# Two heads at a time in SSD and retention, and whole-row products for the last 16 tokens, in a two-layer hybrid decoder trunk

## Chip, cores and metric

The kernel runs on one core of one Trainium2 chip. The metric is device time in microseconds (us), the median of the runs shown. TensorE (PE) does the matrix products; VectorE (DVE), ScalarE (ACT) and GpSimd (POOL) work on tiles; SyncE (SP) issues most loads.

## What is computed

Two layers over 272 tokens (16 learned meta tokens and 256 of the input) of width 1024, all in float32 for its user. Each layer norms its input, projects it, runs four causal token mixers side by side, gates and sums their branch projections, and ends with an out projection and a squared-ReLU MLP. Cut to what matters here:

```python
for l in range(DEPTH):                          # 2
    u = rms_norm(h, norm_pre_mix[l])
    proj = u @ w_in[l]
    y_ret  = retention_mixer(...)   # 4 heads, keys of 64, values of 128, rotary on q and k, fixed decay
    y_s5   = s5_mixer(...)          # 32 groups of 16 channels, 64 complex states each
    y_ssd  = ssd_mixer(...)         # 8 heads of 64 channels in 2 groups, keys of 128, decay from the data
    y_hg   = hgrn2_mixer(...)       # 4 heads, keys and values of 128, a decay for each key channel
    mixed = sum(sigmoid(gate) * branch_projection) @ w_out[l]
    h = h + rms_norm(mixed, norm_post_mix[l])
    m = square(relu(rms_norm(h, norm_pre_mlp[l]) @ w_up[l])) @ w_down[l]
    h = h + rms_norm(m, norm_post_mlp[l])
return h[:, N_META:]
```

For a head with a scalar decay a mixer is y[t] = sum over s <= t of decay(s, t) (q[t] . k[s]) v[s].

## The kernel before

**The stream.** Channels lie on the partitions, tokens along the free dimension. All weights come in 336 chunks of 128 x 1024 in float32 (load on SP, L318). ACT makes the chunk's high part `whi` (L325), DVE its low part `wlo` (L327), both float32r; one chunk gives 24 products, high by high (L344), high by the input's low part (L345), low by high (L347), into one of three banks "g". This stream of products runs through the whole kernel, and what the mixers do comes in between. The chunks of a layer come in the order HGRN2's inputs, SSD's, S5's, gates and branch projections with retention's inputs among them, out projection, MLP.

**The mixers over tokens.** HGRN2, SSD and retention are computed without a recurrence, as a masked 272 x 272 product a head. The tokens are cut into tiles of 128, 128 and 16. `scores` makes k^T q for the three tiles of s against the tokens t from that tile on: 272, 144 and 16 columns, laid side by side as 432. The keys `kpad` are padded with zeros to 384 tokens. `attend` sums v[s]^T P[s, t] over the three tiles: 272, 144 and 16 columns again, the last one with 16 rows of contraction (`v2`, a tile of 16 partitions, and `P[0:16, 416:432]`). float32 products stand as two records each in the trace.

- HGRN2 (`hgrn_in` L1177, `hgrn` L1214) builds P of two heads a tile and attends with 128 value channels.
- SSD (`ssd_in` L1319, `ssd` L1411): a head's decay is itself a product, with 32 rows of the array (L1428, `rows=32`, at row 32 mt); ACT applies Relu and Exp (L1429, L1430), POOL multiplies by the group's masked k^T q (L1431), and `attend` (L1432) gives 64 channels, two heads sharing one bank: `yp[64 * hh:64 * hh + 64]`. DVE adds the skip (L1433).
- Retention (`ret_in` L1465, `ret` L1497): POOL rotates q and k (four products on 32 partitions each, L1482, then L1483, L1486, and L1487 into `kpad`), and PE turns the values to token-major order (`turn`, L694). Heads have 64 rows of keys, two in one tile (L1505); DVE masks (L1507), `attend` (L1509) gives 128 channels.
- S5 (`s5` L1072, `s5_run` L1091) works in four quarters with many small steps on PE, DVE, POOL and ACT; its last step copies its outputs back to channels by tokens (eight copies, L1152) and cuts them in two (L364). POOL and DVE build S5's tables between (L979 to L984, L1003 to L1005).

**What sets the order.** Each engine takes its queue strictly in order. The order within an engine is made at build time by a scheduler that simulates the program, guided by program order and by ranks (`high_priority`) for loads and cuts of chunks; so code that is written in another sequence can move instructions far from it. Two resources tie the mixers together: the two banks "ma" (HGRN2, retention) and the two banks "mb" (SSD, then S5), each handed on in program order, and the 4352-byte slots. In `ssd` the loop over four tiles `mt` takes one bank for the outputs of two heads and one more for each head's scores:

```python
for mt in range(4):
    yp = self.bank("mb")[:, :T]
    for hh in range(2):
        sg = self.bank("mb")[:, :432]
        self.scores(sg, L[hh], R, base=32 * mt, rows=32)
        ...
        self.attend(yp[64 * hh:64 * hh + 64], [v01[:, s, hd] for s in range(2)], v2[:, hd], E)
```

At the start POOL zeroes the padding of `kpad` (L394), and 14 products on those zeros (L398) run on PE while the first loads come in.

## Time and profile before

| | |
|---|---|
| median of 3 runs | 1293.81 us (1292.19 to 1296.15) |
| span of the profiled execution | 1294.5 us, 0.7 above the median |
| PE busy | 1231.3 us (95%) |
| DVE busy | 898.3 us (69%) |
| ACT busy | 695.2 us (54%) |
| POOL busy | 388.4 us (30%) |

The profile is of one execution. Matmuls are pipelined and their ends are modelled, so two products overlap in the trace, and a cost on PE is best read from start to start. In a timeline row the first number is the start in us from the span's start, the second the duration; then engine, line, operation, output <- inputs, for PE the rows * columns of the array, partitions x elements, type and count; a bracket at the end is the idle time before, and what released it.

### The profile page before, as it was taken

To read this page: it belongs to the slowest core of one execution; us is meant where nothing else is said; L and a number is where in the kernel's file an instruction comes from. 1 tells how busy PE (TensorE), PEld (TensorE's weight loads), DVE (VectorE), ACT (ScalarE), POOL (GpSimd) and SP (SyncE) were. 2 spreads that over 40 slices of the span, in tenths; PEclk is the share of its full clock that TensorE was granted. 3 is DMA by queue.
4 is the path that set the end of the run, shared out by engine and by line. 5 is a ranking of instruction groups with operands and counts; after the bars stand their busy time and mean duration, and the time that the engine had idled before them with its cause. 6 is when DMAs were issued, how large, how long until landed. Compare 5 with 4: busy or idle time off the path is not lost.

```text
span 1294.5 us, 24278 instructions
## 1 busy us (share of the span) xinstructions
PE 1231.3 (95%) x9534; PEld 1185.8 (92%) x9534; DVE 898.3 (69%) x1480; ACT 695.2 (54%) x1218; POOL 388.4 (30%) x416
## 2 busy tenths in 40 slices
PE   9999998986999989999989999998999998999997
PEld 8989888885999989999988999998999997999996
DVE  8999958987555775554459795689865486655444
ACT  6446755533465466554445548546536456665442
POOL 2332336686100332210015241265680031322001
PEclk9999999997999999999999999998999999999999
DMA  6423332341345435445443332442343554455552
GB/s 238 154 84 114 112 125 94 103 140 65 115 169 174 172 110 183 172 178 175 170 145 131 121 128 83 154 142 92 115 160 131 188 181 153 153 189 183 188 184 98
DMA packets 53187, 186.69 MB, mean 144 GB/s; under 512 B 6096, under 2 KB 7248, under 8 KB 53072
## 3 DMA queue, kind: packets, MB, share of 16 engines
q1 hardware_dynamic: 50480, 179.40, 40.1%
q10 hardware_dynamic: 2592, 5.74, 1.3%
q8 instruction: 75, 1.23, 0.4%
q14 instruction: 40, 0.33, 0.1%
HBM read 184.06 MB, written 1.05 MB: 143 GB/s over the span
## 4 chain that ended last, share of the span: by engine, by line
PE 70%; DVE 17%; POOL 5%; issue 5%; ACT 2%; DMA 1%; DVEq 0%; SPq 0%; ACTq 0%; POOLq 0%
PE g L347 21%; PE g L345 21%; PE g L344 21%; DVE wlo L327 4%; DMA s5a<-in_bc 1%; DVE S L1152 1%; PE mb L711 1%; POOL S L1482 1%; PE mb L717 1%; DVE S L1395 1%; DVE s5a L1004 1%; DVE h L600 1%; DVE S L1262 1%; PE ma L711 1%; PE ma L717 1%
## 5 line engine op out<-in xcount | busy, mean ns | idle before, releaser
L327 DVE TENSOR_TENSOR wlo<-wst,whi 128x1024 fp32r<-128x1024 f32 x336 | 434.5, 1294 | 244.0 <-PE g L347 209.8
L325 ACT ACTIVATE whi<-wst 128x1024 fp32r<-128x1024 f32 x336 | 355.6, 1059 | 368.8 <-PE g L345 285.4
L347 PE MATMUL g<-xh_u,wlo 128*128 128x272 f32 (+1 forms) x1024 | 301.7, 296 | 16.5 <-DVE wlo L327 16.4
L344 PE MATMUL g<-xh_u,whi 128*128 128x272 f32 (+1 forms) x1024 | 300.3, 294 | 1.3 <-ACT S L654 0.9
L345 PE MATMUL g<-xl_u,whi 128*128 128x272 f32 (+1 forms) x1024 | 298.1, 292 | 0.0
L344 PE MATMUL g<-S,whi 128*128 128x272 f32 (+1 forms) x832 | 236.1, 288 | 4.2 <-ACT S L537 3.7
L347 PE MATMUL g<-S,wlo 128*128 128x272 f32 (+1 forms) x808 | 230.5, 289 | 1.8 <-DVE wlo L327 1.8
L345 PE MATMUL g<-S,whi 128*128 128x272 f32 (+1 forms) x768 | 220.4, 289 | 3.1 <-DVE S L548 3.1
L347 PEld LDWEIGHTS g<-xh_u,wlo 128*128 128x128 f32 x1024 | 196.3, 192 | 20.8 <-DVE wlo L327 18.7
L344 PEld LDWEIGHTS g<-xh_u,whi 128*128 128x128 f32 x1024 | 196.9, 192 | 3.4 <-ACT S L654 1.0
L345 PEld LDWEIGHTS g<-xl_u,whi 128*128 128x128 f32 x1024 | 196.8, 192 | 0.8 <-issue 0.4
L344 PEld LDWEIGHTS g<-S,whi 128*128 128x128 f32 x832 | 157.3, 190 | 5.0 <-ACT S L537 4.2
L347 PEld LDWEIGHTS g<-S,wlo 128*128 128x128 f32 x808 | 152.3, 190 | 2.7 <-DVE wlo L327 2.4
L345 PEld LDWEIGHTS g<-S,whi 128*128 128x128 f32 x768 | 146.0, 190 | 4.9 <-DVE S L548 4.7
L345 PE MATMUL g<-xl_npm,whi 128*128 128x272 f32 (+1 forms) x512 | 148.3, 291 | 2.0 <-DVE xl_npm L548 2.0
L344 PE MATMUL g<-xh_npm,whi 128*128 128x272 f32 (+1 forms) x512 | 143.6, 288 | 2.4 <-ACT xh_npm L537 2.4
L347 PE MATMUL g<-xh_npm,wlo 128*128 128x272 f32 (+1 forms) x496 | 142.6, 288 | 0.0
L345 PEld LDWEIGHTS g<-xl_npm,whi 128*128 128x128 f32 x512 | 98.4, 192 | 2.9 <-DVE xl_npm L548 2.6
L673 POOL TENSOR_TENSOR acc<-acc,tmp 128x272 f32<-128x272 f32 (+1 forms) x48 | 38.0, 807 | 205.4 <-DVE tmp L672 205.4
L344 PEld LDWEIGHTS g<-xh_npm,whi 128*128 128x128 f32 x512 | 96.5, 192 | 3.0 <-ACT xh_npm L537 2.9
L347 PEld LDWEIGHTS g<-xh_npm,wlo 128*128 128x128 f32 x496 | 95.0, 192 | 0.2
L503 POOL TENSOR_TENSOR tmp<-tmp 128x272 f32<-128x272 f32 (+1 forms) x64 | 42.1, 658 | 141.1 <-DVE wlo L327 101.0
(379 smaller groups left out, 2194.4 us busy)
## 6 DMA issues: line engine op xcount, KB each, us to landing
wst<-in_w SPq DMA_DIRECT2D x336, 512.0 KB, 3.5
S<-in_rot ACTq DMA_DIRECT2D x4, 544.0 KB, 5.0
s5a<-in_bc ACTq DMA_DIRECT2D x8, 256.0 KB, 3.7
h<-in_h SPq DMA_DIRECT2D x4, 272.0 KB, 4.8
S<-in_ssdc ACTq DMA_DIRECT2D x2, 384.0 KB, 4.4
dtc<-in_ssdc ACTq DMA_DIRECT2D x2, 272.0 KB, 4.7
out<-h SPq DMA_DIRECT2D x2, 256.0 KB, 2.5
S<-in_lvl SPq DMA_DIRECT2D x1, 448.0 KB, 7.7
```

The costliest lines, as they stand in the source:

```text
L325: a = nc.scalar.activation(hi, st, AF.Copy)
L327: nc.vector.tensor_tensor(out=lo, in0=st, in1=hi.bitcast(F32), op=ALU.subtract)
L344: self.nc.tensor.matmul(out, lhsT=a, rhs=r, start=st, stop=False)
L345: self.nc.tensor.matmul(out, lhsT=a, rhs=s, start=False, stop=False)
L347: end = self.nc.tensor.matmul(out, lhsT=b, rhs=r, start=False, stop=en)
L503: nc.gpsimd.tensor_tensor(out=q, in0=a, in1=a, op=ALU.mult)
L600: e.tensor_tensor(out=self.h[:, k, sl], in0=self.h[:, k, sl], in1=mw[:, k], op=ALU.add)
L673: nc.gpsimd.tensor_tensor(out=a, in0=a, in1=t, op=ALU.add)
L711: nc.tensor.matmul(ps[:, c0:c0 + T - q0], lhsT=k[b, 128 * s:128 * s + 128], rhs=q[b, q0:T], start=True, stop=True)
L717: nc.tensor.matmul(out[:, 0:T], lhsT=v01[0], rhs=P[:, 0:272], start=True, stop=False)
L1004: e.tensor_tensor(out=tmp, in0=X[1 - r], in1=F[1], op=ALU.mult)
L1152: nc.vector.tensor_copy(o, i)
```

## The change

- `scores` and `attend` take several heads at once. The loop over the three token tiles is outside, the heads inside, so that the products of two heads follow each other: on different rows of the array for scores (SSD's 32 rows of two tiles, retention's 64 rows), on different columns for SSD's attends.
- The last 16 tokens go over all 128 rows. `v2` is no longer a tile of 16 partitions but a view of one of two persistent tiles `vpad` (128 x 512), zeroed once by POOL at the start, ahead of `kpad`: the first serves HGRN2 and retention, the second SSD. HGRN2's P gets its columns 416 to 432 zeroed by POOL in each layer.
- `ssd` loops over the two groups and, within, over the two heads of a tile: the scores of two tiles take two banks "mb"; then each tile takes one bank for its outputs. Before, an output bank was taken ahead of the scores.
- `ret` takes two banks "ma" for a pair's scores, and its output banks now from "mb".

Comments are gone as well, so line numbers shift by some 5 to 15.

```diff
+        self.vpad = [self.cp.tile([128, 512], F32, name=f"vpad{i}") for i in range(2)]
+        for t in self.vpad:
+            nc.gpsimd.memset(t, 0.0)
         for t in self.kpad:
             nc.gpsimd.memset(t[:, :, T:384], 0.0)
...
-    def scores(self, ps, k, q, base=0, rows=128):
+    def scores(self, *many, rows=128):
         nc = self.nc
-        b = slice(base, base + rows)
         for s, (c0, q0) in enumerate(((0, 0), (272, 128), (416, 256))):
-            nc.tensor.matmul(ps[:, c0:c0 + T - q0], lhsT=k[b, 128 * s:128 * s + 128], rhs=q[b, q0:T], start=True,
-                             stop=True)
+            for ps, k, q, base in many:
+                b = slice(base, base + rows)
+                nc.tensor.matmul(ps[:, c0:c0 + T - q0], lhsT=k[b, 128 * s:128 * s + 128], rhs=q[b, q0:T], start=True,
+                                 stop=True)
-    def attend(self, out, v01, v2, P):
+    def attend(self, *many):
         nc = self.nc
-        nc.tensor.matmul(out[:, 0:T], lhsT=v01[0], rhs=P[:, 0:272], start=True, stop=False)
-        nc.tensor.matmul(out[:, 128:T], lhsT=v01[1], rhs=P[:, 272:416], start=False, stop=False)
-        nc.tensor.matmul(out[:, 256:T], lhsT=v2, rhs=P[0:16, 416:432], start=False, stop=True)
+        for s, (t, p0) in enumerate(((0, 0), (128, 272), (256, 416))):
+            for out, v01, v2, P in many:
+                nc.tensor.matmul(out[:, t:T], lhsT=v01[s] if s < 2 else v2, rhs=P[:, p0:p0 + T - t], start=s == 0,
+                                 stop=s == 2)
...
-        v01, v2 = self.slot(4, [128, 2, 4, 128]), self.t1([16, 4, 128], tag="v2", bufs=2)
+        v01, v2 = self.slot(4, [128, 2, 4, 128]), self.vpad[0].rearrange("p (i e) -> p i e", i=4)
...
+        for P in PP:
+            g.memset(P[:, :, 416:432], 0.0)
...
-        for mt in range(4):
-            yp = self.bank("mb")[:, :T]
-            EE = self.slot(13 + mt % 2, [128, 2, 432])
+        for gr in range(2):
+            mts = (2 * gr, 2 * gr + 1)
+            EE = [self.slot(13 + mt % 2, [128, 2, 432]) for mt in mts]
             for hh in range(2):
-                hd = 2 * mt + hh
-                sg = self.bank("mb")[:, :432]
-                self.scores(sg, L[hh], R, base=32 * mt, rows=32)
-                E = EE[:, hh]
-                nc.scalar.activation(E, sg, AF.Relu, scale=-1.0)
-                self.decay = nc.scalar.activation(E, E, AF.Exp, scale=-1.0)
-                g.tensor_tensor(out=E, in0=E, in1=sm[:, mt // 2], op=ALU.mult)
-                self.attend(yp[64 * hh:64 * hh + 64], [v01[:, s, hd] for s in range(2)], v2[:, hd], E)
-            v.scalar_tensor_tensor(out=yt[:, mt], in0=xs[:, mt], scalar=self.hf(l, "sd")[:, mt:mt + 1], in1=yp,
-                                   op0=ALU.mult, op1=ALU.add)
+                sg = [self.bank("mb")[:, :432] for _ in mts]
+                self.scores(*[(p, L[hh], R, 32 * mt) for p, mt in zip(sg, mts)], rows=32)
+                for p, ee in zip(sg, EE):
+                    E = ee[:, hh]
+                    nc.scalar.activation(E, p, AF.Relu, scale=-1.0)
+                    self.decay = nc.scalar.activation(E, E, AF.Exp, scale=-1.0)
+                    g.tensor_tensor(out=E, in0=E, in1=sm[:, gr], op=ALU.mult)
+            for ee, mt in zip(EE, mts):
+                yp = self.bank("mb")[:, :T]
+                self.attend(*[(yp[64 * hh:64 * hh + 64], [v01[:, s, 2 * mt + hh] for s in range(2)], v2[:, 2 * mt + hh],
+                               ee[:, hh]) for hh in range(2)])
+                v.scalar_tensor_tensor(out=yt[:, mt], in0=xs[:, mt], scalar=self.hf(l, "sd")[:, mt:mt + 1], in1=yp,
+                                       op0=ALU.mult, op1=ALU.add)
...
-        for hd in range(4):
-            ps = self.bank()[:, :432]
-            self.scores(ps, k[:, hd // 2], q[:, hd // 2], base=64 * (hd % 2), rows=64)
-            P = PP[hd // 2][:, hd % 2]
-            nc.vector.tensor_tensor(out=P, in0=ps, in1=self.c("m432"), op=ALU.mult)
-            yp = self.bank()[:, :T]
-            self.attend(yp, [v01[:, s, hd] for s in range(2)], v2[:, hd], P)
+        for pair in range(2):
+            ps = [self.bank()[:, :432] for _ in range(2)]
+            self.scores(*[(p, k[:, pair], q[:, pair], 64 * i) for i, p in enumerate(ps)], rows=64)
+            for i, p in enumerate(ps):
+                nc.vector.tensor_tensor(out=PP[pair][:, i], in0=p, in1=self.c("m432"), op=ALU.mult)
+            for i in range(2):
+                hd = 2 * pair + i
+                yp = self.bank("mb")[:, :T]
+                self.attend((yp, [v01[:, s, hd] for s in range(2)], v2[:, hd], PP[pair][:, i]))
```

How the order of the built program moves is shown at three places. The first is PE in layer 0, at the first attend of SSD. Before, the products of one head (`mb_1364`; L717 to L719 are its 272, 144 and 16 columns) stand in one place, with two of HGRN2's head norms (L725, L726) among them:

```order
L344 MATMUL g_2409<-xh_u_154,whi_2412 128x272
L717 MATMUL mb_1364<-S_122_1365,S_113_1333 64x272
L718 MATMUL mb_1364<-S_122_1365,S_113_1333 64x144
L725 MATMUL ma_927<-tmp_928,onesr 128x272
L726 MATMUL ma_927<-sq_929,onesr 128x272
L725 MATMUL ma_935<-tmp_936,onesr 128x272
L726 MATMUL ma_935<-sq_937,onesr 128x272
L719 MATMUL mb_1364<-S_122_1365,v_114_1334 64x16
```

In the change a head's 272 columns (`mb_1398`, the same line L726 for all) come 20 rows ahead of this place, alone; here are the second head's 272 and the 144 and 16 columns of both:

```order
L345 MATMUL g_2445<-xl_u_159,whi_2448 128x272
L726 MATMUL mb_1398<-S_119_1368,S_112_1338 64x272
L726 MATMUL mb_1398<-S_119_1368,S_112_1338 64x144 x2
L726 MATMUL mb_1398<-S_119_1368,vpad_92 64x16 x2
L347 MATMUL g_2445<-xh_u_158,wlo_2449 128x272
```

So the attends of a tile are two visits of the stream, with the columns of both heads next to each other in the second one only.

The second place is DVE in layer 0, at the end of S5. Before, the cut of S5's output (L364), the copies back (L1152) and the cuts of chunks (L327) stand in this order:

```order
L1140 TENSOR_TENSOR S_96_1020<-mb_2219,S_200_2200 128x272
L1005 TENSOR_TENSOR s5b_2982<-s5b_2982,s5a_2973 128x4x128
L364 TENSOR_TENSOR S_203_2251<-S_145_1815,S_202_2250 128x272 x2
L327 TENSOR_TENSOR wlo_3486<-wst_3483,whi_3485 128x1024
L1152 COPY S_145_1815<-S_96_1020 32x136 x8
L327 TENSOR_TENSOR wlo_3524<-wst_3521,whi_3523 128x1024
L364 TENSOR_TENSOR S_203_2251<-S_145_1815,S_202_2250 128x272 x2
L327 TENSOR_TENSOR wlo_3561<-wst_3558,whi_3560 128x1024
```

In the change (the copies are L1160):

```order
L1013 TENSOR_TENSOR s5b_2986<-s5b_2986,s5a_2977 128x4x128
L327 TENSOR_TENSOR wlo_3333<-wst_3330,whi_3332 128x1024
L364 TENSOR_TENSOR S_201_2255<-S_143_1819,S_200_2254 128x272 x2
L1160 COPY S_143_1819<-S_95_1025 32x136 x8
L327 TENSOR_TENSOR wlo_3365<-wst_3362,whi_3364 128x1024
L364 TENSOR_TENSOR S_201_2255<-S_143_1819,S_200_2254 128x272
L327 TENSOR_TENSOR wlo_3413<-wst_3410,whi_3412 128x1024
L364 TENSOR_TENSOR S_201_2255<-S_143_1819,S_200_2254 128x272
```

The tail of S5 stands three cuts of chunks earlier in DVE's queue, and a cut stands between its last two pieces.

The third place is POOL in layer 0, around the rotary products of retention. Before (L1482 to L1487 are rotary work, L983, L984 and L1003 to L1005 tables of S5 for the next layer):

```order
L983 TENSOR_TENSOR s5e_2985<-s5ea,s5eb 128x288
L984 TENSOR_TENSOR s5e_2985<-s5e_2985 128x288
L1482 TENSOR_TENSOR S_260_3395<-S_253_3260,S_259_3390 32x1088 x4
L1003 TENSOR_TENSOR s5c_2983<-s5a_2973,s5p 128x4x128
L1004 TENSOR_TENSOR s5d_2984<-s5a_2973,s5p 128x512
L1122 MEMSET s5d_2984 128x8
L1483 TENSOR_TENSOR S_253_3260<-S_253_3260,S_258_3389 128x1088
L1005 TENSOR_TENSOR s5c_2983<-s5c_2983,s5d_2984 128x4x128
L1486 TENSOR_TENSOR S_261_3401<-S_253_3260,S_260_3395 128x544
L1487 TENSOR_TENSOR kpad_89<-S_253_3260,S_260_3395 128x2x272
```

In the change (rotary work is L1496 to L1501, tables L1011 to L1013):

```order
L1011 TENSOR_TENSOR s5c_2987<-s5a_2977,s5p 128x4x128
L1012 TENSOR_TENSOR s5d_2988<-s5a_2977,s5p 128x512
L1130 MEMSET s5d_2988 128x8
L1013 TENSOR_TENSOR s5c_2987<-s5c_2987,s5d_2988 128x4x128
L274 COPY S_256_3393<-S_251_3264 128x1
L274 COPY S_257_3394<-S_251_3264 128x1
L1045 MEMSET s5d_2988 32x4x32
L1045 MEMSET s5d_2988 32x4x64
L1045 MEMSET s5d_2988 32x4x96
L1496 TENSOR_TENSOR S_258_3399<-S_251_3264,S_257_3394 32x1088 x4
L1497 TENSOR_TENSOR S_251_3264<-S_251_3264,S_256_3393 128x1088
L1500 TENSOR_TENSOR S_259_3405<-S_251_3264,S_258_3399 128x544
```

All tables of S5 stand ahead of the rotary products now; before, some stood among them.

## Rows read from the trace of the kernel before

**Rows 1.** The page's first line and its part 1: busy, share, instructions.

```profile
span 1294.5 us, 24278 instructions
...
PE 1231.3 (95%) x9534; PEld 1185.8 (92%) x9534; DVE 898.3 (69%) x1480; ACT 695.2 (54%) x1218; POOL 388.4 (30%) x416
```

**Rows 2.** Timeline of PE, layer 0: the stream, and SSD's group scores on the whole array.

```profile
117.02 0.29 PE L344 MATMUL g<-xh_u,whi 128*128 128x272 f32 x1
117.14 0.29 PE L345 MATMUL g<-xl_u,whi 128*128 128x272 f32 x1
...
118.27 0.99 PE L711 MATMUL mb<-S,kpad 128*128 128x272 f32 x6
119.11 0.37 PE L345 MATMUL g<-xl_u,whi 128*128 128x272 f32 x1
```

**Rows 3.** Windows: start:end, length, busy and count by engine, granted clock, DMA share, GB/s.

```profile
177.00:285.00 108.00, 97.10 (x723) 90.99 (x722) 89.31 (x131) 51.09 (x93) 67.11 (x72) 0.96 0.34 113
285.00:325.00 40.00, 28.10 (x167) 25.70 (x167) 31.68 (x26) 14.15 (x33) 26.33 (x19) 0.76 0.22 74
```

**Rows 4.** Timeline of PE, layer 0: an attend of HGRN2, and the next head's first product.

```profile
120.07 0.62 PE L717 MATMUL ma<-S,S 128*128 128x272 f32 x2
...
120.87 0.39 PE L719 MATMUL ma<-S,v 16*128 16x16 f32 x2
121.19 0.73 PE L717 MATMUL ma<-S,S 128*128 128x272 f32 x2
```

**Rows 5.** Timeline of PE, layer 0: an attend of SSD, and the next head's first product.

```profile
148.38 0.67 PE L717 MATMUL mb<-S,S 128*64 128x272 f32 x2
148.89 0.41 PE L718 MATMUL mb<-S,S 128*64 128x144 f32 x2
149.23 0.28 PE L719 MATMUL mb<-S,v 16*64 16x16 f32 x2
149.44 0.67 PE L717 MATMUL mb<-S,S 128*64 128x272 f32 x2
```

**Rows 6.** Timeline of PE, layer 0: scores of an SSD head in the stream.

```profile
144.01 0.29 PE L345 MATMUL g<-xl_u,whi 128*128 128x272 f32 x1
144.22 0.51 PE L711 MATMUL mb<-S 32*128 32x272 f32 x3
...
144.89 0.29 PE L344 MATMUL g<-xh_u,whi 128*128 128x272 f32 x1
```

**Rows 7.** Timeline of PE, layer 0: scores of a retention head in the stream.

```profile
329.06 0.29 PE L347 MATMUL g<-yh_ssd,wlo 128*128 128x272 f32 x1
329.28 1.09 PE L711 MATMUL ma<-S,kpad 64*128 64x272 f32 x6
...
330.54 0.29 PE L345 MATMUL g<-yl_ssd,whi 128*128 128x272 f32 x1
```

**Rows 8.** Timeline of POOL at the start: the padding of the keys.

```profile
0.73 0.50 POOL L394 MEMSET kpad<- 128x224 f32 x2 [0.29 <-POOLq L1525]
```

**Rows 9.** Timeline of PE, 285 to 325 us: the two long waits.

```profile
302.17 0.59 PE L347 MATMUL g<-xh_u,wlo 128*128 128x272 f32 x1 [6.45 <-DVE wlo L327]
...
311.70 0.59 PE L347 MATMUL g<-xh_u,wlo 128*128 128x272 f32 x1 [4.18 <-DVE wlo L327]
```

**Rows 10.** Timeline of DVE, layer 0: the end of S5.

```profile
294.75 5.36 DVE L364 TENSOR_TENSOR S<-S,S 128x272 fp32r<-128x272 f32 x2
...
302.14 8.25 DVE L1152 COPY S<-S 32x136 f32<-32x136 f32 x8
```

**Rows 11.** Timeline of POOL, layer 0: the rotary products.

```profile
288.49 11.31 POOL L1482 TENSOR_TENSOR S<-S,S 32x1088 f32<-32x1088 f32 x4
```

**Rows 12.** Timeline of DVE, layer 1: the same copies at the end of S5.

```profile
933.21 2.38 DVE L1152 COPY S<-S 32x136 f32<-32x136 f32 x8
```

**Rows 13.** Timeline of POOL, layer 0: a multiply of SSD and the table work behind it.

```profile
159.93 1.55 POOL L1431 TENSOR_TENSOR S<-S,early 128x432 f32<-128x432 f32 x1
161.44 2.25 POOL L1005 TENSOR_TENSOR s5c<-s5c,s5d 128x512 f32<-128x512 f32 x1
```

More of the change, by code (lines that the diff above doesn't have):

```diff
@@ L1209, in hgrn_in @@
             v.scalar_tensor_tensor(out=fm, in0=ps, scalar=0.5, in1=r, op0=ALU.mult, op1=ALU.mult)
-            self.tokens(fm, None, v01[:, :, i], v2[:, i])
+            self.tokens(fm, None, v01[:, :, i], v2[0:16, i])
         norm()
@@ L1294, in hgrn @@
                 yp = self.bank()[:, :T]
-                self.attend(yp, [v01[:, s, hd] for s in range(2)], v2[:, hd], P[:, i])
+                self.attend((yp, [v01[:, s, hd] for s in range(2)], v2[:, hd], P[:, i]))
                 nc.scalar.activation(kg[:, i], yp, AF.Square)
@@ L1399, in ssd_in @@
             v.scalar_tensor_tensor(out=o, in0=th, scalar=1.0, in1=ac, op0=ALU.add, op1=ALU.mult)
-        v01, v2 = self.slot(10, [128, 2, 8, 64]), self.t1([16, 8, 64], tag="v2", bufs=2)
+        v01, v2 = self.slot(10, [128, 2, 8, 64]), self.vpad[1].rearrange("p (h e) -> p h e", h=8)
         for s in range(3):
@@ L1406, in ssd_in @@
                 self.turn(tp[:, i], xs[:, i, 128 * s:128 * s + n])
-            v.tensor_tensor(out=v01[:, s] if s < 2 else v2, in0=tp.rearrange("p i (h e) -> p (i h) e", h=2),
+            v.tensor_tensor(out=v01[:, s] if s < 2 else v2[0:16], in0=tp.rearrange("p i (h e) -> p (i h) e", h=2),
                             in1=dk[0:n, s].unsqueeze(2).to_broadcast([n, 8, 64]), op=ALU.mult)
@@ L1418, in ssd @@
             ps = self.bank("mb")[:, :432]
-            self.scores(ps, bm[:, gr], cm[:, gr])
+            self.scores((ps, bm[:, gr], cm[:, gr], 0))
             v.tensor_tensor(out=sm[:, gr], in0=ps, in1=self.c("m432"), op=ALU.mult)
-        for mt in range(4):
-            yp = self.bank("mb")[:, :T]
-            EE = self.slot(13 + mt % 2, [128, 2, 432])
+        for gr in range(2):
+            mts = (2 * gr, 2 * gr + 1)
+            EE = [self.slot(13 + mt % 2, [128, 2, 432]) for mt in mts]
             for hh in range(2):
-                hd = 2 * mt + hh
-                sg = self.bank("mb")[:, :432]
-                self.scores(sg, L[hh], R, base=32 * mt, rows=32)
-                E = EE[:, hh]
-                nc.scalar.activation(E, sg, AF.Relu, scale=-1.0)
-                self.decay = nc.scalar.activation(E, E, AF.Exp, scale=-1.0)
-                g.tensor_tensor(out=E, in0=E, in1=sm[:, mt // 2], op=ALU.mult)
-                self.attend(yp[64 * hh:64 * hh + 64], [v01[:, s, hd] for s in range(2)], v2[:, hd], E)
-            v.scalar_tensor_tensor(out=yt[:, mt], in0=xs[:, mt], scalar=self.hf(l, "sd")[:, mt:mt + 1], in1=yp,
-                                   op0=ALU.mult, op1=ALU.add)
+                sg = [self.bank("mb")[:, :432] for _ in mts]
[11 more added lines that the diff above has]
+                                       op0=ALU.mult, op1=ALU.add)
         return yt
@@ L1487, in ret_in @@
         g.tensor_tensor(out=k[:, :, 0:T], in0=qk[:, 2:4], in1=sw[:, 2:4], op=ALU.add)
-        v01, v2 = self.slot(0, [128, 2, 4, 128]), self.t1([16, 4, 128], tag="v2", bufs=2)
+        v01, v2 = self.slot(0, [128, 2, 4, 128]), self.vpad[0].rearrange("p (i e) -> p i e", i=4)
         for i in range(4):
@@ L1492, in ret_in @@
             nc.scalar.activation(fm, ps, AF.Copy)
-            self.tokens(fm, self.c("cen"), v01[:, :, i], v2[:, i])
+            self.tokens(fm, self.c("cen"), v01[:, :, i], v2[0:16, i])
         return q, k, v01, v2
```

4 lines of the change are left out of this document (2 added, 2 removed).

## The prediction, made before the change was run

> **What bounds the kernel now.** I read the page first. The span is 1294.5 us and TensorE (PE) is busy for 1231.3 of them [rows 1], so what the other engines cost is found only where PE stands or runs slowly. The others are VectorE (DVE), ScalarE (ACT) and GpSimd (POOL). In the steady stream two products of a chunk start 0.12 to 0.13 us apart (117.02, 117.14) [rows 2]; a chunk has 24 of them, some 3.0 us, in which DVE has one low part to cut.
>
> So there are two kinds of gain to look for: PE's own time in the mixers' float32 products, and stretches in which PE waits. For the first I read PE's timeline by starts, since ends are modelled: a visit of the stream to other products costs the distance between the start of its first instruction and that of the next stream product. For the second I cut the first layer into stages with the windows view. In 177 to 285 us (S5's stage) PE is busy 97.1 of 108.0 us, and in 285 to 325 us only 28.1 of 40.0, at a mean granted clock of 0.76 of full speed [rows 3]. The second of these is the worst stretch of the mixers, and the change moves the work around it.
>
> **The change part by part.**
>
> *The last 16 tokens with all rows.* Three products of the same column counts (272, 144, 16) on the whole array take 0.84 us (118.27 to 119.11) [rows 2]. An HGRN2 head with its 16-row last product takes 1.12 us (120.07 to 121.19), of which the last product alone takes 0.32 (120.87 to 121.19) [rows 4]. The rhs there has 16 columns, so what it pays is the change to 16 rows and back. With zeros the head should cost what the whole-array products do: 1.12 - 0.84 = 0.28 saved, for 16 heads (4 of HGRN2 and 4 of retention, two layers; retention's have the same shapes) **-4.5 us**. Ends: 0 and 16 x 0.32 = -5.1.
>
> *SSD's attends.* A head takes 1.06 us (148.38 to 149.44), its last product 0.21 of that [rows 5]. On all rows it should at best come to the 0.84 of the whole array, so 0.22 x 16 heads = -3.5, if nothing overlaps. If the two heads of a tile ran side by side on columns 0 to 63 and 64 to 127, a head's whole cost would go: 8 x 1.06 = -8.5. The order shows that the scheduler puts the first head's 272 columns by itself, some 20 rows ahead of the rest, so only the 144s and the 16s are neighbours, and each pair pays for two visits. I take **-3.0**; ends 0 and -8.5.
>
> The Trainium skill (TensorE: Matmul & The Clock Gate, The mechanism) says that a weight load runs beside products in flight only where the row group differs; two heads on the same rows and other columns would then gain nothing by lying together. No row of the kernel before has such neighbours, so nothing here shows it; by that rule the term would be the -3.5 without overlap.
>
> *SSD's scores* (32 rows). Between the stream products before and after lie 0.88 us (144.01 to 144.89), of which two stream steps are 0.25: 0.63 for a visit [rows 6]. In the order the two heads' products are mostly still apart or one behind the other, in 7 visits instead of 8 in layer 0. I take **-0.5**; ends 0 and, with every pair at the price of one head, 8 x 0.63 = -5.0.
>
> *Retention's scores* (64 rows). One visit costs 330.54 - 329.06 - 0.25 = 1.23 us [rows 7]. Of the four pairs the second one of each layer now is interleaved, the first is spread over three visits. I take **-0.7**; ends 0 and 4 x 1.23 = -4.9.
>
> *Start.* POOL now zeroes two 128x512 tiles ahead of the kpad memset, 0.50 us for 2 x 224 elements a partition [rows 8], for which PE's warm-up waits. By size that is 0.50 x 1024 / 448 = 1.1 us; the first real product waits for other things, so only a shorter warm-up reaches the path. I take **+0.3**; ends 0 and +1.1. The memsets of P's last 16 columns are small and lie in POOL's slack.
>
> *What the order moves.* SSD now asks for its banks "mb" in another sequence and ends some 120 PE rows earlier; S5, which uses the same two banks, starts and ends some 97 rows earlier, and at the tail's end the stream has about 90 more products before retention's turns. This matters at 285 to 325 us. There PE waits twice for a low part, 6.45 and 4.18 us [rows 9]. The releaser named is DVE's cut, but the cut stood behind S5's tail: two L364 that take 5.36 us and eight small copies that take 8.25 us [rows 10]. Beside the first POOL runs the four rotary products (11.31 us) [rows 11], beside the copies the rest of the rotary work and S5's tables. The same eight copies take 2.38 us in the second layer, where they come ahead of the rotary work [rows 12]. So DVE and POOL slow each other there, and the price is paid by PE's queue, first by standing and then by the half clock. In the new order of POOL all of S5's work precedes the rotary products, and on DVE the tail stands three cuts earlier, with the cuts between its pieces. I expect the collision to go. Its price: idle 40.0 - 28.1 = 11.9 us is the lower count. The upper: 167 PE records at 0.126 are 21 us of 40, so up to 19 lost [rows 3]. I take **-14**, a little over the lower count, since some wait for the keys will remain; ends 0 and -19. The next late thing is kpad's add at the end of the rotary chain, for which retention's scores wait; its cover is the 100 products between turns and scores (12 us).
>
> *S5's stage.* In layer 0 it loses 108.0 - 97.1 = 10.9 us [rows 3] to hand-overs among DVE, POOL and PE; for the second layer I assume the same. All of it is reshuffled: earlier, against other stream products. I see no reason for a sign: **0**, with ends of -8 and +8 (most of what it loses now, either way).
>
> Sum: -4.5 - 3.0 - 0.5 - 0.7 + 0.3 - 14 = -22.4. From the profiled 1294.5 that is 1272.1; the median of the runs, 1293.81, stands 0.7 below the profiled execution, so the forecast is **1271.4 us**. The MLP, the out projection and SP's loads keep their order.
>
> **Rivals.**
>
> *A: only PE's own time is saved.* The tail's loss is put off: DVE and POOL have the same work to do in the first layer, and DVE was busy 89.3 of 108 us already before the tail [rows 3]. If S5 simply ends as late as before because its own chain sets its pace, the tail meets the rotary work again and only -8.4 stays: 1293.8 - 8.4 = 1285.4. For it: three cuts earlier are only some 9 us of the stream. Against: POOL's order now forbids rotary work before S5's last tables. Chance 0.20.
>
> *B: slower, by the wait for a pair.* PE takes its queue in order, and the first attend of a tile now waits until both score banks of a group have been through ScalarE and POOL. POOL's multiply took 1.55 us and stood beside S5 table work, an instruction of which took 2.25 [rows 13]. If two such pieces come ahead of a pair's last multiply, PE stands some 3.8 us, and with 8 pairs in the two layers that is 30 us. With the direct gain and half of the tail's: 1293.8 - 8.4 - 7 + 30 = 1308. It decides where the chain is longer than the stream products between scores and attend, about 45 x 0.126 = 5.7 us; in the order there are mostly more than that. Chance 0.08.
>
> *C: the pairs do run side by side.* Where the products of two heads are neighbours, the second costs nearly nothing: 8 x 0.34 = 2.7 for SSD's 144s (148.89 to 149.23 [rows 5]) and 2 x 1.23 = 2.5 for the two interleaved retention pairs [rows 7], together 5.2, of which 0.7 is in the sum: 4.5 more, about 1267. With all of them adjacent, the ends above, it would be 1257, but the order keeps most of them apart. Chance 0.10. The Trainium skill (TensorEngine Tiling (Array Packing), Key Properties) says that different tiles work independently, loads and products alike; that is the rule for this case.
>
> *D: the change is not what it says.* The scheduler splits the pairs again: true for most of SSD's scores by the order, and already in the sum. If the shifted S5 stage gives back what the tail gains (its +8 end and the first-layer tail at a half), the time is 1293.8 - 8.4 - 7 + 8 + a few, some 1288 to 1293, no change. Chance 0.07.
>
> **How the numbers follow.** A measurement of this kernel tells about 0.3%, 3.9 us, from no change: faster is below 1289.9, slower above 1297.7. The forecast's case has 0.55, A 0.20, B 0.08, C 0.10, D 0.07. Faster: 0.55 + 0.10 and most of A, 0.18, together 0.83; slower is B, 0.08; the rest, 0.09, is no change. The range goes from 1258 (C's side, the tail at its upper end) to 1289 (A with part of its gain lost); outside it are B, D and little else.
>
> **What would show it.** After the change: an HGRN2 head at about 0.84 us from start to start; its last product at 0.05 rather than 0.32. No PE wait above 2 us between S5's end and retention's scores, the eight copies at about 2.4 us and a granted clock near 1.00 in that stretch: then the tail's term is right. SSD's neighbouring 144s starting closer than 0.15 us speak for C. PE waits on SSD's attends, released by POOL, speak for B. A wait of over 4 us on a low part behind L364 or the copies speaks for A. The prediction is wrong where the first layer's mixers are less than 10 us shorter, or the second's not shorter at all.

## The result, and the profile after

The changed kernel takes **1277.8 us**, the kernel before 1293.4 (medians). The ratio, estimated over the runs, is 0.9867, 95% interval 0.9846 to 0.9888, so 1.3% faster. One of the change's four runs went at a granted clock of 0.55 and took 1930.6 us, and the ratio leaves it out. The prediction of 1271.4 us (1258 to 1289, faster) holds it in its range and has the sign; it is 6.4 us too low.

The profiled execution is a typical one of its kernel (1277.7 us, 1.8 of them outside the span). That of before, with its span of 1294.5, was about 1296, the slowest of its runs; so the profiles differ by 18.6 us, the medians by 15.6, and every difference to before that is read from traces below may hold up to 3 us too much. (The prediction's 0.7 us between profile and median compares a span with a time; the forecast is the same, 1293.8 - 22.4.)

The page after, first line and part 1, beside [rows 1]:

```profile
span 1275.9 us, 24312 instructions
...
PE 1216.1 (95%) x9534; PEld 1174.6 (92%) x9534; DVE 893.0 (70%) x1480; ACT 694.2 (54%) x1219; POOL 411.0 (32%) x422
```

PE is busy 15.2 us less; its share stays. The windows of the same stretches of the stream, beside [rows 3]:

```profile
175.00:285.00 110.00, 93.85 (x702) 89.64 (x702) 98.87 (x142) 54.30 (x106) 75.41 (x80) 0.95 0.34 114
285.00:305.00 20.00, 20.00 (x153) 18.67 (x152) 11.17 (x8) 9.04 (x19) 19.59 (x7) 0.99 0.36 127
```

The stretch that took 40 us takes 20, with PE busy throughout at a clock of 0.99. The row above it has 16 us idle instead of 11, and DVE busy for 99 of 110 us. But the two rows hold the same part of the stream and not the same work: in the change S5 ends 18 us before 285, and what follows it lies in the first row. So here is S5 from its first product to its last one (called S5's own stretch below), in layer 0 and in layer 1, and the stretch behind it in layer 0. Before:

```profile
190.40:287.90 97.50, 86.60 (x642) 81.62 (x640) 85.19 (x124) 44.42 (x81) 67.17 (x72) 0.95 0.34 113
287.90:325.00 37.10, 25.20 (x150) 22.80 (x150) 28.81 (x24) 14.15 (x33) 23.58 (x17) 0.77 0.20 71
836.80:930.40 93.60, 86.39 (x672) 82.73 (x671) 85.38 (x125) 47.05 (x86) 58.40 (x68) 0.95 0.34 120
```

After:

```profile
170.40:266.90 96.50, 85.23 (x661) 81.47 (x660) 89.14 (x129) 45.87 (x86) 65.97 (x70) 0.98 0.30 102
266.90:305.00 38.10, 33.22 (x233) 31.45 (x233) 25.46 (x28) 19.55 (x41) 29.02 (x18) 0.91 0.44 151
808.70:902.60 93.90, 83.41 (x637) 79.14 (x636) 81.96 (x117) 44.63 (x83) 62.66 (x68) 0.93 0.35 114
```

In layer 0 S5 takes as long as before and PE idles as much (11 us). In layer 1 PE idles 10.5 us instead of 7.2. Behind S5 in layer 0 PE idles 4.9 us instead of 11.9, in two waits for a low part that stand behind S5's last steps on DVE:

```profile
273.49 0.39 PE L347 MATMUL g<-xh_u,wlo 128*128 128x272 f32 x1 [2.19 <-DVE wlo L327]
279.21 0.59 PE L347 MATMUL g<-xh_u,wlo 128*128 128x272 f32 x1 [2.69 <-DVE wlo L327]
```

To place the gain I took the starts of the stream's products (L344, L345, L347) in all traces, counted from the program's start: the same number is the same product. The new order also moves S5 against the stream, so the gain is cut at S5's own first and last product. The columns are the numbers of the stream's products between which S5 stands in layer 0; how long its own stretch takes; what is won or lost ahead of it, in it, and behind it up to product 1440; and three places in the stream, 1440 (behind the long waits of before), 4032 (the end of layer 0) and 5760 (layer 1's mixers done). All times are in us; the first row has before's own, the others the differences to it (a minus is time won). A stretch that has more or fewer stream products than before's is charged 0.125 us for each, an estimate from [rows 2].

```
kernel              S5 stands at   it takes   ahead    in it   behind    1440     4032     5760
before                960-1366       97.5     190.4     97.5     28.8    316.7    677.5    996.7
the change            852-1277       96.5      -6.5     -3.4     -9.0    -18.9    -20.8    -18.7
rows_only             960-1366       97.3      -3.2     -0.2      0.0     -3.4     -4.4     -7.5
pairs_only            852-1277       98.6      -5.2     -1.3    -13.6    -20.1    -20.9    -17.5
no_alternation        854-1232       95.5      -4.1     +1.5    -10.4    -12.9    -13.4     -9.9
no_rotary_products    960-1366       98.3      -1.2     +0.7    -11.6    -12.1    -12.1    -12.2
old_ssd_loop          960-1366       98.1      -4.5     +0.6     -0.5     -4.4     -5.1     -9.4
old_ret_loop          852-1277       96.5      -4.9     -3.4    -11.7    -20.0    -20.8    -19.5
joint_exp             876-1281       94.2      -7.7     -3.2     -8.3    -19.3    -21.1    -21.8
joint_exp_first       864-1273       95.0      -4.7     -2.9    -11.2    -18.8    -19.3    -20.1
new_loop_layer0       852-1277       97.9      -6.3     -2.0    -11.7    -20.0    -21.9    -26.0
copies_on_scalar      852-1202       95.2      +2.3     +4.7    -10.5     -3.5     -5.5    +11.2
layer0_and_copies     852-1202       95.8      -0.5     +5.2    -10.3     -5.6     -7.5     +5.1
fewer_cuts            852-1241       89.1      -4.3     -6.3    -11.3    -21.9    -22.4    -21.6
```

The program of new_loop_layer0 is that of the change up to here in layer 0 on all engines; its shares differ by up to 2.7 us and its sum at 1440 by 1.1, so that is how much single traces scatter. The profile of joint_exp lies 3.2 us below that kernel's median, that of copies_on_scalar 7.8 above.

So the change wins 18.9 us up to product 1440 of layer 0: 9.0 behind S5, where the clash was, 6.5 ahead of S5 and 3.4 in its own stretch. It wins 1.9 in the rest of layer 0 and loses 2.1 in layer 1, where old_ssd_loop, without the move of S5, wins 4.3.

The tail of S5 on DVE, beside [rows 10], and the rotary products on POOL, beside [rows 11]:

```profile
273.36 1.87 DVE L364 TENSOR_TENSOR S<-S,S 128x272 fp32r<-128x272 f32 x2
275.24 2.66 DVE L1160 COPY S<-S 32x136 f32<-32x136 f32 x8
```

```profile
285.08 13.78 POOL L1496 TENSOR_TENSOR S<-S,S 32x1088 f32<-32x1088 f32 x4 [8.50 <-ACT S L1489]
```

The tail is over before the rotary products begin: 1.87 instead of 5.36 us, 2.66 instead of 8.25. The rotary products did not get faster (13.78 us beside DVE's cuts of chunks), but there PE has no wait left.

HGRN2's attends on whole rows, beside [rows 4], SSD's second visit for a tile, beside [rows 5], two SSD heads' scores, beside [rows 6], and two of retention's, beside [rows 7]. PE's timeline after:

```profile
118.61 0.95 PE L726 MATMUL ma<-S,S 128*128 128x272 f32 x4
119.40 0.29 PE L726 MATMUL ma<-S,vpad 128*128 128x16 f32 x2
119.54 0.37 PE L347 MATMUL g<-xh_u,wlo 128*128 128x272 f32 x1
...
131.17 0.28 PE L344 MATMUL g<-xh_u,whi 128*128 128x272 f32 x1
131.38 0.52 PE L717 MATMUL mb<-S 32*128 32x272 f32 x6
131.83 0.39 PE L345 MATMUL g<-xl_u,whi 128*128 128x272 f32 x1
132.06 0.28 PE L347 MATMUL g<-xh_u,wlo 128*128 128x272 f32 x1
...
138.40 0.29 PE L345 MATMUL g<-xl_u,whi 128*128 128x272 f32 x1
138.62 0.67 PE L726 MATMUL mb<-S,S 128*64 128x272 f32 x4
138.92 0.24 PE L726 MATMUL mb<-S,vpad 128*64 128x16 f32 x2
139.12 0.41 PE L726 MATMUL mb<-S,S 128*64 128x144 f32 x2
139.37 0.24 PE L726 MATMUL mb<-S,vpad 128*64 128x16 f32 x2
139.54 0.39 PE L347 MATMUL g<-xh_u,wlo 128*128 128x272 f32 x1
139.77 0.29 PE L344 MATMUL g<-xh_u,whi 128*128 128x272 f32 x1
...
321.78 1.10 PE L717 MATMUL ma<-S,kpad 64*128 64x272 f32 x12
322.81 0.39 PE L347 MATMUL g<-xh_u,wlo 128*128 128x272 f32 x1
```

The 16-column product takes 0.14 us (119.40 to 119.54) where it took 0.32. The scores of two SSD heads, six products (on 32 rows one record each), lie between stream products 0.89 us apart (131.17 to 132.06), as three did in [rows 6]. SSD's second visit (one head's 272, both heads' 144 and 16) costs 139.77 - 138.40 - 0.25 = 1.12 us. Two retention heads, alternating, take 1.03 us (321.78 to 322.81), as one did before (329.28 to 330.31; [rows 7] leaves out the second of these rows):

```profile
330.31 0.39 PE L344 MATMUL g<-yh_ssd,whi 128*128 128x272 f32 x1
```

### The profile page after: what moved, and what is told of

It reads as the page before. It is cut to its first block, busy times and chain, and to the rows that moved or that the text cites. A ratio compares the mean times of both kernels' runs of the same rounds, so it can differ in the third digit from the quotient of the medians.

```text
span 1275.9 us, 24312 instructions
## 1 busy us (share of the span) xinstructions
PE 1216.1 (95%) x9534; PEld 1174.6 (92%) x9534; DVE 893.0 (70%) x1480; ACT 694.2 (54%) x1219; POOL 411.0 (32%) x422
## 3 DMA queue, kind: packets, MB, share of 16 engines
q8 instruction: 75, 1.23, 0.4%
## 4 chain that ended last, share of the span: by engine, by line
PE 76%; DVE 13%; issue 4%; POOL 3%; ACT 2%; DMA 1%; SPq 0%; DVEq 0%; ACTq 0%; POOLq 0%
PE g L347 22%; PE g L344 22%; PE g L345 22%; DVE wlo L327 3%; PE mb L726 1%; PE ma L1263 1%; PE mb L717 1%; POOL S L1496 1%; DVE h L604 1%; DMA s5a<-in_bc 1%; DVE big_npom L601 1%; DVE s5a L1012 1%; ACT whi L325 1%; PE ma L726 1%; PE mb L1109 1%
## 5 line engine op out<-in xcount | busy, mean ns | idle before, releaser
L327 DVE TENSOR_TENSOR wlo<-wst,whi 128x1024 fp32r<-128x1024 f32 x336 | 438.5, 1306 | 259.1 <-PE g L347 220.8
L347 PE MATMUL g<-xh_u,wlo 128*128 128x272 f32 (+1 forms) x1024 | 299.7, 294 | 16.0 <-DVE wlo L327 15.8
L344 PE MATMUL g<-xh_u,whi 128*128 128x272 f32 (+1 forms) x1024 | 299.5, 293 | 0.6 <-ACT early L1068 0.4
L345 PE MATMUL g<-xl_u,whi 128*128 128x272 f32 (+1 forms) x1024 | 297.8, 291 | 0.0
L344 PE MATMUL g<-S,whi 128*128 128x272 f32 (+1 forms) x832 | 236.0, 288 | 4.6 <-ACT S L541 4.1
L347 PE MATMUL g<-S,wlo 128*128 128x272 f32 (+1 forms) x808 | 230.0, 288 | 1.7 <-DVE wlo L327 1.7
L345 PE MATMUL g<-S,whi 128*128 128x272 f32 (+1 forms) x768 | 220.4, 289 | 2.2 <-DVE S L552 1.9
L347 PEld LDWEIGHTS g<-xh_u,wlo 128*128 128x128 f32 x1024 | 195.7, 192 | 21.0 <-DVE wlo L327 18.2
L344 PEld LDWEIGHTS g<-xh_u,whi 128*128 128x128 f32 x1024 | 196.5, 192 | 2.6 <-ACT early L1068 0.7
L345 PEld LDWEIGHTS g<-xl_u,whi 128*128 128x128 f32 x1024 | 196.5, 192 | 1.5 <-issue 1.2
L344 PEld LDWEIGHTS g<-S,whi 128*128 128x128 f32 x832 | 157.1, 190 | 5.3 <-ACT S L541 4.5
L347 PEld LDWEIGHTS g<-S,wlo 128*128 128x128 f32 x808 | 151.9, 189 | 2.6 <-DVE wlo L327 2.2
L345 PEld LDWEIGHTS g<-S,whi 128*128 128x128 f32 x768 | 145.8, 190 | 4.1 <-DVE S L552 4.0
L345 PE MATMUL g<-xl_npm,whi 128*128 128x272 f32 (+1 forms) x512 | 147.7, 291 | 1.2 <-DVE xl_npm L552 1.2
L344 PE MATMUL g<-xh_npm,whi 128*128 128x272 f32 (+1 forms) x512 | 143.6, 289 | 2.4 <-ACT xh_npm L541 2.4
L347 PE MATMUL g<-xh_npm,wlo 128*128 128x272 f32 (+1 forms) x496 | 140.5, 288 | 0.0
L345 PEld LDWEIGHTS g<-xl_npm,whi 128*128 128x128 f32 x512 | 99.1, 193 | 1.9 <-DVE xl_npm L552 1.7
L344 PEld LDWEIGHTS g<-xh_npm,whi 128*128 128x128 f32 x512 | 96.7, 193 | 2.9 <-ACT xh_npm L541 2.9
L347 PEld LDWEIGHTS g<-xh_npm,wlo 128*128 128x128 f32 x496 | 94.2, 192 | 0.2
L507 POOL TENSOR_TENSOR tmp<-tmp 128x272 f32<-128x272 f32 (+1 forms) x64 | 45.7, 714 | 137.3 <-DVE wlo L327 79.5
```

The lines of the kernel that those rows point to most:

```text
L327: nc.vector.tensor_tensor(out=lo, in0=st, in1=hi.bitcast(F32), op=ALU.subtract)
L344: self.nc.tensor.matmul(out, lhsT=a, rhs=r, start=st, stop=False)
L345: self.nc.tensor.matmul(out, lhsT=a, rhs=s, start=False, stop=False)
L347: end = self.nc.tensor.matmul(out, lhsT=b, rhs=r, start=False, stop=en)
L507: nc.gpsimd.tensor_tensor(out=q, in0=a, in1=a, op=ALU.mult)
```

## The experiments

Costs "per visit" are worked as in the prediction: from the stream product before to the second one behind, less two steps of 0.125 us and less idle time. Sums of PE's visits are over the visits with scores or attends of SSD and retention or attends of HGRN2, in both layers; they hang by about 1 us on how visits with other products among them are counted.

**rows_only** puts the whole-row tail alone into the kernel before.

```diff
-        nc.tensor.matmul(out[:, 256:T], lhsT=v2, rhs=P[0:16, 416:432], start=False, stop=True)
+        nc.tensor.matmul(out[:, 256:T], lhsT=v2, rhs=P[:, 416:432], start=False, stop=True)
```

> The kernel before with only the whole-row tail of the attends (two zeroed tiles, P's zeroed columns); heads still one at a time, so the order of the instructions stays that of the kernel before. Theory (the shift of S5 and the direct saving are two separate things): the direct saving of this part alone, 16 heads of HGRN2 and retention x 0.28 = 4.5 us and 16 heads of SSD x about 0.16 = 2.6 us, so 1286 to 1288 us, and the two long waits before retention (6.45 and 4.18 us) are still there. Rival (most of the gain of the whole change is the whole-row tail): 1280 us or less. Second rival (zeros cost what they save): 1293 us.

Measured: 1288.5 us (ratio 0.9961, 0.9946 to 0.9976), half a us above its range, and the waits of 6.45 and 4.29 us are there. A pair of HGRN2 heads went from 2.45 to 1.86 us, a lone SSD head from 1.26 to 1.12. The whole-row tail of the attends is worth its own saving, 5.4 us, and does not move S5.

**pairs_only** is the change with the 16-row tail.

```diff
-                nc.tensor.matmul(out[:, t:T], lhsT=v01[s] if s < 2 else v2, rhs=P[:, p0:p0 + T - t], start=s == 0,
+                nc.tensor.matmul(out[:, t:T], lhsT=v01[s] if s < 2 else v2, rhs=(P if s < 2 else P[0:16])[:, p0:p0 + T - t], start=s == 0,
```

> The changed kernel with the 16-row tail of the kernel before (v2 on 16 partitions, no zeroed tiles), heads in pairs and the new loop in SSD; the order is that of the changed kernel. Theory: S5 still ends early and the two long waits of layer 0 stay away, so only the tail's direct saving is lost against the changed kernel, 5 to 8 us: 1282 to 1286 us. Rival (the whole-row tail is what counts): 1290 us or more.

Measured: 1279.4 us (0.9893, 0.9874 to 0.9912), 1.6 above the change by the medians and some 3 by the ratios, less than expected. PE's visits cost 4.6 us more in all, but in layer 0 product 1440 comes no later (-20.1 against -18.9 in the table). The same whole-row tail that gave 5.4 us in the old order gives 2 to 3 in the new one, by intervals that overlap.

**no_alternation** exchanges the loops in `scores` and `attend`.

```diff
-        for s, (t, p0) in enumerate(((0, 0), (128, 272), (256, 416))):
-            for out, v01, v2, P in many:
+        for out, v01, v2, P in many:
+            for s, (t, p0) in enumerate(((0, 0), (128, 272), (256, 416))):
```

> The changed kernel with the loops over heads and token tiles exchanged in scores and attend: a head's three products come one after the other, then the next head's; banks, zeros and the loop of SSD as in the change, the order of everything else nearly the same. Theory (two heads on other rows or columns run side by side only where a product of the one follows a product of the other, and the alternation gives that): 2 to 5 us slower than the changed kernel, 1279 to 1283 us. Rival (alternation gives nothing beside mere neighbourhood): within 1 us of the changed kernel's 1277.8.

Measured: 1288.0 us (0.9955, 0.9940 to 0.9970), 10 above the change. That is more than either theory said, and the premise did not hold: the scheduler moved S5 too, whose own stretch now has 378 stream products instead of 425. By the table 2.4 us are lost ahead of S5 and 4.9 in its stretch, against the change. What is left of the comparison are single visits: an SSD head's attend, now whole, takes 1.10 to 1.23 us, so a tile some 2.3 against the change's 2.0; two neighbouring scores on 32 rows take 0.64 us here too, without alternation.

**no_rotary_products** leaves out POOL's four rotary products of layer 0 in the kernel before.

```diff
-        for q in range(4):
+        for q in range(4 if l else 0):
```

> The kernel before without GpSimd's four rotary products (32 partitions x 1088) in layer 0; the sine table stands in for their result, so layer 0's retention is another function. Everything up to the end of S5 keeps the order of the kernel before. Theory (the long waits of layer 0 come from VectorE's last S5 steps and these products slowing each other): the two L364 take about 0.8 us and not 5.4, the eight copies 2.4 to 4 and not 8.25, the two waits of 6.45 and 4.18 us on the low part shrink under 2 us each, and the kernel takes 1272 to 1282 us. Rival (VectorE's queue is late by itself at S5's end): the waits stay above 3 us and the time above 1288 us.

Measured: 1284.2 us (0.9925, 0.9908 to 0.9941). DVE's timeline:

```profile
291.71 2.83 DVE L364 TENSOR_TENSOR S<-S,S 128x272 fp32r<-128x272 f32 x2
294.46 2.36 DVE L327 TENSOR_TENSOR wlo<-wst,whi 128x1024 fp32r<-128x1024 f32 x1
296.86 3.65 DVE L1152 COPY S<-S 32x136 f32<-32x136 f32 x8
```

The waits of 10.6 us shrink to 2.1, and 11.6 us are won behind S5, in the order of the kernel before. The copies and waits are as the theory has them; L364 keeps 2.83 us, beside POOL's remaining work; the time lies 2 us above its range. So the clash is worth 11 to 12 us by itself. The change, with 4.9 us of waits left, wins 9.0 in that place; new_loop_layer0, the same program there, wins 11.7, and the others with SSD's new loop in layer 0 win 8.3 to 13.6.

**old_ssd_loop** and **old_ret_loop** undo the two new loops one at a time.

```diff
-        for gr in range(2):
-            mts = (2 * gr, 2 * gr + 1)
+        for mt in range(4):
+            yp = self.bank("mb")[:, :T]
...
-        for pair in range(2):
-            ps = [self.bank()[:, :432] for _ in range(2)]
+        for hd in range(4):
+            ps = self.bank()[:, :432]
```

> The changed kernel with SSD's loop as before (one head after the other, the output bank taken ahead of the scores); whole-row tails and retention's pairs stay. Theory (it is SSD's new loop over the banks that ends SSD early and with it brings S5 forward): the order up to S5's end is that of the kernel before, the two waits of over 4 us on the low part before retention are back, and the time is that of the whole-row tail alone less 1 to 2 us for retention's interleaved pair: 1285 to 1289 us. Rival (retention's output banks or the zeros bring the gain): 1280 us or less.

> The changed kernel with retention's loop as before (one head after the other, banks all from ma); SSD's new loop and the whole-row tails stay. Theory: S5's place and the missing long waits stay as in the change; lost is only what retention's pairs gave on the array, by the trace two interleaved pairs at 1.1 us instead of 2.2 and two spread ones at 2.7 instead of 2.4, so 1 to 2 us in all: 1278 to 1281 us. Rival (retention's pairing carries several us): 1284 us or more.

Measured: 1288.3 us (0.9956, 0.9938 to 0.9973) and 1277.5 us (0.9871, 0.9856 to 0.9887). Without SSD's new loop the long waits are back (9.1 us in two); PE's timeline of old_ssd_loop, beside [rows 9]:

```profile
297.79 0.60 PE L347 MATMUL g<-xh_u,wlo 128*128 128x272 f32 x1 [4.88 <-DVE wlo L327]
```

Without retention's new loop S5 stands at the same products and the time stays as it was in the change, though PE's visits cost some 2 us more. The shift of S5 comes from SSD's loop alone.

**joint_exp** makes the two heads' weights of an SSD tile in one Exp and one multiply, **joint_exp_first** also ranks the scores earlier.

```diff
-                    self.decay = nc.scalar.activation(E, E, AF.Exp, scale=-1.0)
-                    g.tensor_tensor(out=E, in0=E, in1=sm[:, gr], op=ALU.mult)
+            for ee in EE:
+                self.decay = nc.scalar.activation(ee, ee, AF.Exp, scale=-1.0)
+                g.tensor_tensor(out=ee, in0=ee, in1=sm[:, gr].unsqueeze(1).to_broadcast([128, 2, 432]), op=ALU.mult)
```

> The changed kernel with one Exp and one multiply on GpSimd for the two heads of an SSD tile, so that both heads' weights come at the same moment and the six attends of a tile stand together in PE's queue. Theory (columns run side by side, and what the change loses is the second visit): an SSD tile's attends take about 1.3 us in one visit instead of 0.85 + 1.12; 8 tiles, so some 5 us less on PE, of which layer 0's half is lost in S5's stage, which VectorE sets: 1273 to 1277 us. Rival (the later weights put SSD's end and S5 off): 1280 us or more.

> As joint_exp, and SSD's and retention's scores rank 400 ahead of their place, so that more of the two heads' scores stand together. Theory (rows run side by side wherever the two heads are neighbours): up to 8 x 0.63 = 5 us of SSD's scores and 3 us of retention's less on PE than in the change, part of it lost in S5's stage: 1270 to 1276 us. Rival (what PE saves there is absorbed by the engines behind, and the moved order decides): no better than joint_exp, or worse.

Measured: 1278.6 us (0.9877, 0.9857 to 0.9897) and 1277.8 us (0.9887, 0.9861 to 0.9914): neither is better than the change. On the array the first does what was wanted; PE's timeline of joint_exp:

```profile
163.18 0.29 PE L345 MATMUL g<-xl_u,whi 128*128 128x272 f32 x1
163.39 0.93 PE L726 MATMUL mb<-S,S 128*64 128x272 f32 x8
164.15 0.24 PE L726 MATMUL mb<-S,vpad 128*64 128x16 f32 x4
164.32 0.39 PE L347 MATMUL g<-xh_u,wlo 128*128 128x272 f32 x1
164.55 0.29 PE L344 MATMUL g<-xh_u,whi 128*128 128x272 f32 x1
```

All six products of a tile take 164.55 - 163.18 - 0.25 = 1.12 us, what one head alone takes in rows_only (1.10 to 1.12); there a tile whose heads lie in one visit, mostly one behind the other, takes 1.79. PE's visits fall by some 7 us against the change. Yet a lead of 1.2 us over the change ahead of S5 in layer 0 (-7.7 against -6.5) is 0.4 at product 1440, and a lead of 2.8 us over old_ret_loop is gone there. Differences of 1 us lie within the scatter of the traces, but the 7 us of PE's visits show in neither median.

**new_loop_layer0** uses SSD's new loop in layer 0 only.

```diff
-        for gr in range(2):
...
+        if l == 0:
+            for gr in range(2):
...
+        else:
+            for mt in range(4):
```

> The changed kernel with SSD's new loop in layer 0 only; layer 1 has the loop of the kernel before, with whole-row tails and retention's pairs. Layer 0 keeps the order of the change. Theory (S5's place is worth 17 us in layer 0, where it ends the clash with the rotary work, and costs some 6 us in layer 1, where there was no clash): layer 1 gains as in old_ssd_loop, about 4 us, where the change loses 2: 1270 to 1274 us. Rival (layer 1's loss has another cause, such as retention's output banks): 1276 us or more.

Measured: **1271.2 us** (0.9821, 0.9805 to 0.9838), the best version here, 6.6 below the change. PE's waits in layer 1, 760 to 930 us (the first three kinds: us in all, times, longest), of the change and of this kernel:

```profile
PE g L347 <- DVE wlo L327: 4.9, 3, 1.9
PE g L344 <- DVE acc L673: 3.2, 2, 2.6
PE mb L1109 <- DVE S L1148: 2.4, 2, 1.7
```

```profile
PE mb L696 <- DVE s5g L1013: 2.0, 2, 1.0
PE g L347 <- DVE wlo L327: 1.9, 3, 0.8
PE mb L1146 <- DVE s5d L1134: 1.4, 2, 0.8
```

With SSD's old loop, and so with S5 in its old place, layer 1 wins 4.1 us (from -21.9 to -26.0), where the change loses 2.1.

**copies_on_scalar** gives ACT the half of S5's small copies that DVE had; **layer0_and_copies** adds this to new_loop_layer0.

```diff
-                if q % 2:
-                    nc.vector.tensor_copy(o, i)
-                else:
-                    nc.scalar.activation(o, i, AF.Copy)
+                nc.scalar.activation(o, i, AF.Copy)
```

> The changed kernel with VectorE's half of S5's small copies (8 ahead of S5 and 2 x 8 behind its quarters in each layer) on ScalarE, which did the other half. Theory (VectorE's work sets when S5 ends, so time saved on PE ahead of it is lost, and time saved on VectorE counts): some 6 us less on VectorE a layer, S5 in layer 0 ends 4 to 6 us earlier, 1267 to 1274 us. Rival (the hand-overs among the engines set it, not VectorE's load): within 2 us of the change, or slower where ScalarE's queue delays a chunk's high part.

> Both of the edits new_loop_layer0 and copies_on_scalar. Theory: they add up, 1263 to 1270 us. Rival (the copies' move only reshuffles S5's stage): no better than new_loop_layer0.

Measured: 1299.1 us (1.0036, 1.0020 to 1.0052) and 1300.6 us (1.0053, 1.0037 to 1.0068): slower than the kernel before. In copies_on_scalar, against the change, 8.8 us are lost ahead of S5, where ACT now has 16 copies of 0.69 us in its queue at SSD's exponentials (that these cost the time was not tried), and 8.1 in S5's stretch, where the scheduler has put 350 stream products instead of 425. S5 itself took 95.2 us, 1.3 less than in the change. Since the order moved, this says little on what sets S5's end.

**fewer_cuts** leaves out DVE's cut of every second of 16 chunks in S5's stage.

```diff
+            cut = self.wi not in range(38, 54, 2)
+            lo = self.wp.tile([128, 1024], F32R, tag="wlo", bufs=NLO, name=f"wlo{self.wi}") if cut else hi
```

> The changed kernel without VectorE's low-part cut of every second one of 16 chunks in S5's stage of layer 0 (chunks 38 to 52); their third products take the high part instead, so those 8 chunks give another result. These cuts are no part of S5's own chain. In the change 21 cuts took 31.7 us of that stage, so 8 of them 12 us of VectorE. Theory (VectorE's work sets when S5's stage ends): the stage ends 7 to 12 us earlier, 1266 to 1271 us. Rival (S5's hand-overs among VectorE, GpSimd and TensorE set it): less than 3 us, 1275 us or more.

Measured: 1273.9 us (0.9836, 0.9812 to 0.9860), 3.9 below the change; in the trace S5's own stretch takes 89.1 us instead of 96.5 and S5 ends 5.2 us earlier, while DVE is busy for 78.5 us in it instead of 89.1. That lies between the two theories. DVE's load sets part of S5's end: of 12 us taken off DVE, 7 came off S5's stretch, 5 reached its end and 4 the time. What sets the rest, the hand-overs among DVE, POOL and PE or the moved order, is open.

## Why the prediction was right, and where not

- *Whole rows.* Right per head: 0.28 us forecast for HGRN2, 0.29 measured. SSD's heads gave 0.14 rather than the 0.22 of the upper reckoning.
- *SSD's attends.* -3.0 was taken; a tile went from 2.5 us (or 2.4 in one visit) to some 2.0, so about -4. The reason differs in part: the neighbours do run side by side, and the second visit eats half of it. The sum by the rule on row groups that the prediction weighed from the Trainium skill (TensorE: Matmul & The Clock Gate, The mechanism) does not hold here: two heads on the same rows and other columns took 1.12 us, one alone 1.10 to 1.12. What the prediction cites from the Trainium skill (TensorEngine Tiling (Array Packing), Key Properties), that different tiles work independently, agrees with these rows.
- *Scores.* SSD's two neighbours cost one, as in rival C, but only one or two pairs a layer stand so: the -0.5 was about right. Retention was -0.7 in the sum; undoing it costs PE some 2 us of visits.
- Over all visits PE went from some 62 to some 54 us: about -8, forecast -8.7. *Start*: the first product came 0.39 us later, forecast 0.3.
- *What the order moves.* Right in cause, large in size. The clash of S5's tail with the rotary work went, and the chip run without the rotary products shows that it was the clash that PE paid for (11.6 us). The forecast was -14; behind S5 the change won 9.0 and its repeat in new_loop_layer0 11.7. Of the signs that the prediction named, the copies came as forecast (2.66 us), but two PE waits of over 2 us stayed, and the clock from S5's end to 305 us was 0.91.
- *S5's stage*: this step failed. "I see no reason for a sign: 0" was said of both layers, and their sum is near 0 by luck: in S5's own stretch layer 0 won 3.4 us and layer 1 lost 3.9. In layer 1 S5 took as long as before (93.9 against 93.6 us), but only 401 stream products went by in that time instead of 430. Worked as in the table, that stretch is 0.1 to 0.8 us better than before's in the four kernels with SSD's old loop in layer 1 (rows_only, no_rotary_products, old_ssd_loop, new_loop_layer0), and 1.1 to 3.9 worse in the seven that have the new one there and leave S5's copies alone: so it is SSD's loop that costs it. Through which wait is open. PE waits there on `acc`, 3.2 us, which is new; but the merge's eight `acc` adds on DVE lie in S5's stretch before and after.
- *Ahead of S5* layer 0 won 6.5 us, more than the prediction's terms for PE's own time up to there, some 2.6 (four HGRN2 heads, half of the SSD terms, the start); rows_only won 3.2. PE idles 1.0 us less there (4.7 for 5.7); where the rest comes from is open.
- The prediction's own mark for a wrong prediction, a second layer that is not shorter at all, was met. The total stayed in the range since what was short behind S5 and in layer 1 was in part made up ahead of S5 and in its stretch in layer 0.
- Of the rivals, *B* did not come: in the change PE sits idle ahead of none of SSD's attends. *A* had one true half: S5 sets its own pace. Its stretch in layer 0 takes 94.2 to 98.6 us in every kernel that leaves DVE's cuts and S5's copies alone, whatever PE saves. But with the new loop it begins 20 us earlier, and so it ends 21 us earlier. And PE's saving is not the kernel's: between old_ret_loop and joint_exp PE's visits differ by some 9 us, and the times by 1 the other way.

## What to carry to other kernels

The whole-row tail of the attends, a change to PE's instructions alone, was worth 5.4 us here. The reshuffle of the order that came with SSD's new loop was worth 14.5 in one layer (-18.9 against -4.4 without it) and cost 6.4 in the other (+2.1 against -4.3): compare the order of the two programs first, and look for what the moved block now lies over. Measure a moved block by its own first and last instruction, not by a fixed place in the stream: by the fixed windows S5's stage had seemed to get 5 us worse in layer 0. PE time saved was not time of the kernel here where another chain set the pace. Where a change helps one layer by its place and harms the next, make it for the one alone: that was the best version.

## What the runs showed of the hardware

Two float32 heads on different columns of the same rows cost what one costs, if their products alternate (1.12 against 1.10 to 1.12 us), and 1.79 us in one visit where they mostly lie one head behind the other. Two on different groups of 32 rows do so alternating or not (0.64 against 0.63), and two on 64 rows, alternating (1.03 against 1.03). Whether two heads on 64 rows do so without alternation was not tried.

POOL's multiplies and DVE's work on the same stretch slow each other. Eight copies on DVE took 8.25, 3.65 and 2.66 us as POOL's work beside them shrank; of the first eight, five beside POOL's multiplies took 1.10 to 2.43 us each, and the last three, with POOL idle, 0.28. In the change POOL's last rotary add (L1501) took 2.34 us in layer 0, almost all of it beside DVE's work, and 1.36 in layer 1, where 0.34 us of it were.
